# Seven block products for eight in 14 of the 44 weight-tile pairs of the second feed-forward product

## The chip, the cores and the metric

The kernel runs on one core of one Trainium2 chip. The metric is the device time of one execution in microseconds (us). TensorE multiplies matrices, VectorE and ScalarE work on rows of 128 partitions in SBUF and PSUM, GpSimd can do such work too, and SyncE issues the transfers from HBM. TensorE writes only to PSUM, which has eight banks of 128 x 512 numbers.

## The reference

One decoder layer on 256 tokens of width 2048: a token mixer (mLSTM heads and dilated attention), cross-attention into 256 memory tokens, and a SwiGLU feed-forward part. Each of the three is followed by `x = layer_norm(alpha * x + y)` with alpha = 2 ** 0.25. What matters here is the last:

```python
def swiglu_ffn(x, w1, w3, w2):          # x (256, 2048), w1 and w3 (2048, 5632), w2 (5632, 2048)
    return (jax.nn.silu(x @ w1) * (x @ w3)) @ w2
...
    y = swiglu_ffn(x, w1[l], w3[l], w2[l])
    x = layer_norm(DEEPNORM_ALPHA * x + y, ln_g[l, 2], ln_b[l, 2])
```

## The kernel before

All products are computed from float32 values that are split in two: a high part (`SC.copy`, a cast to float32r on ScalarE) and a low part (the value less the high part, a subtraction on VectorE). A product is three matmuls: high x high, high x low and low x high. In a token product (`gemm_tokens`) the transposed activations are the stationary operand, 128 x 128, and a weight tile of 128 rows and 1024 columns moves past it, 512 columns at a time.

The second feed-forward product multiplies the hidden values (`hT`, 44 tiles of 128 features, kept as 22 pairs with both parts) by `w2`. It is done in four pieces. `w2a0` and `w2a1` take the first 24 feature tiles, for the left and the right 1024 output columns; they stand in the middle of the first product, after its piece `f10`. `w2b0` and `w2b1` take the other 20 tiles and come last, before the layer norm. A piece accumulates in four PSUM banks: two halves of the tokens (m) by two halves of its 1024 columns (c). Per weight tile that is 2 x 2 x 3 = 12 matmuls.

`weights` loads the tiles in pairs of 1 MB (three raw buffers, `RAW`) and splits each tile into a pair of buffers `wh` and `wl` (five of each, `SPLIT`). In the last piece the final eight tiles (`LAG2`) are kept in buffers of their own, so that the second token half can follow when the first is already being normed. After a piece `add` puts its four banks into the residual tiles `z`, with the factor alpha in the first pieces and 1.0 in the last; `Norm.add` then takes the statistics too.

`hidden` makes two feature pairs of `hT` from the banks of the first product: silu on ScalarE, a multiplication on VectorE, four transposes on TensorE into a short-lived PSUM bank, and `hT.put`, which splits it. PSUM is shared out as five banks for accumulation (`bank`) and three short-lived ones (`sbank`). SBUF space beside the weight buffers is 34 slots of 128 x 1024, given out in turn (`big`, `slot`, `free`).

The program is written with a scheduler that orders the instructions of each engine ahead of the run, by the order of the text and by when it expects an operand or a buffer to be ready; it also picks the buffers and sets the semaphores. Each engine then works in that order.

Of the kernel before, what the change touches and what calls it, by code (L numbers as in the profile page):

```python
# [35 lines left out]
NSLOT, RAW, SPLIT = 34, 3, 5  # L36
LAG, HEAD, LAG2 = 6, 6, 8
WARM = 2


QM, KM, VM, OM, GI, QA, KA, VA = 0, 1024, 2048, 3072, 4096, 4104, 5128, 6152
# [7 lines left out]
def decoder_layer(ctx: ExitStack, tc: tile.TileContext, A):  # L49
# [48 lines left out]
    def bank(name):  # L98
        return pg.tile([P, 512], F32, tag="g", name=name)
# [18 lines left out]
    class Operand:  # L118


        def __init__(self, name):
            self.name, self.parts = name, {}

        def views(self, j):
            if j not in self.parts:
# [4 lines left out]
        def put(self, j, src):  # L130

            split(*self.views(j), src.rearrange("p (s t) -> p s t", s=2))

        def free(self, j):
            free(self.parts.pop(j))

        def get(self, kt, x, a=0, n=S):
            at = (kt % 2) * 512 + x * S + a
# [30 lines left out]
                split(wh, wl, w[:, s])  # L169
                yield 2 * n + s, wh, wl  # L170

    def weights(src, n, name, load=None, kept=()):

        for b in range(n // 2):
            if load:
                load(b if n == KT else 2 * b)
            first = load is not None and b == 0
            w = wp.tile([P, 2, W], F32, tag="w", name=f"{name}w{b}", bufs=RAW)
            if first:
                for c in range(2):  # L180
                    cs = slice(c * 512, (c + 1) * 512)
                    nc.sync.dma_start(out=w[:, 0, cs], in_=src[b][:, 0, cs])
                if n < KT:
                    load(1)
                nc.sync.dma_start(out=w[:, 1], in_=src[b][:, 1])
            else:
                nc.sync.dma_start(out=w, in_=src[b])
            for i in range(2):
                at = 2 * b + i
                if load and n < KT:  # L190
                    load(at)
                if at in kept:
                    wh, wl = big(f"{name}h{at}"), big(f"{name}l{at}")
                else:
                    wh = wp.tile([P, W], F32R, tag="wh", name=f"{name}h{at}")
                    wl = wp.tile([P, W], F32R, tag="wl", name=f"{name}l{at}")
                eng = G if at in kept and kept[0] == 0 else V
                halves = (slice(0, 512), slice(512, 1024))
                for cs in halves if at in kept or first and i == 0 else (slice(0, 1024),):
                    SC.copy(wh[:, cs], w[:, i, cs])  # L200
                    eng.tensor_tensor(out=wl[:, cs], in0=w[:, i, cs], in1=as_f32(wh[:, cs]), op=ALU.subtract)  # L201
                yield at, wh, wl

    def gemm_tokens(op, src, nkt, name, order=None, kept=range(0), load=None, last=False, steps=None):

        banks = [[bank(f"{name}b{m}{c}") for c in range(2)] for m in range(2)]
        order = order or list(range(nkt))  # L210

        def products(m, n, wh, wl, cols=range(2)):
            xh, xl = (op.get(order[n], x, m * P, P) for x in (0, 1))
            for c in cols:
                cs = slice(c * 512, (c + 1) * 512)
                T.matmul(banks[m][c], xh, wh[:, cs], start=n == 0, stop=False)  # L216
                T.matmul(banks[m][c], xh, wl[:, cs], start=False, stop=False)  # L217
            for c in cols:
                cs = slice(c * 512, (c + 1) * 512)
                T.matmul(banks[m][c], xl, wh[:, cs], start=False, stop=n == nkt - 1)  # L220

        behind = []
        for n, wh, wl in steps or weights(src, nkt, name, load, kept):
            products(0, n, wh, wl)
            if n in kept:
                behind.append((n, wh, wl))
            else:
                products(1, n, wh, wl)
            if kept and n == kept[-1]:
                for c in range(2):  # L230
                    for i, wh, wl in behind:
                        products(1, i, wh, wl, (c,))
                for _, wh, wl in behind:
                    free(wh, wl)
            if last and n % 2 and n not in kept:
                op.free(order[n] // 2)
        if last:
            for n in kept:
                if n % 2:
                    op.free(order[n] // 2)  # L240
        return banks

    def gemm_features(op, src, name, load=None, last=False):
# [277 lines left out]
    def add(m, g, banks, scale=ALPHA):  # L521
        for c in range(2):
            t = z[m][2 * g + c]
            V.scalar_tensor_tensor(out=t, in0=t, scalar=scale, in1=banks[m][c], op0=ALU.mult, op1=ALU.add)

    class Norm:


# [242 lines left out]
    def hidden(j, banks, parts, name):  # L771

        for i in range(2):
# [8 lines left out]
            for s in range(2):  # L782
                for m in range(2):
                    T.transpose(
                        pt[:, s * S + m * P : s * S + (m + 1) * P], hs[m][:, s * P : (s + 1) * P], ident
                    )
            hT.put(j + i, pt)
            free(*hs)

    banks = gemm_tokens(x2, A["w13_tokens"], KT, "f0", kept=range(HEAD))  # L790
# [1 line left out]
    n, half = FFN // 256, 12  # L792

    def w2_first():
        for c in range(2):
            banks = gemm_tokens(hT, A["w2"][c][:half], 2 * half, f"w2a{c}", last=c == 1)
            for m in range(2):
                add(m, c, banks)

    for g in range(2, n, 2):  # L800
        pair = weights_of_pair(A["w13"][g - 2 : g], f"f{g}")
# [4 lines left out]
    ln = Norm(2, "l2")  # L806
    order = list(range(2 * half, HT))
    nkt = len(order)
    banks = gemm_tokens(hT, A["w2"][0][half:], nkt, "w2b0", order)
    for m in range(2):  # L810
        ln.add(m, 0, banks, scale=1.0)
    banks = gemm_tokens(hT, A["w2"][1][half:], nkt, "w2b1", order, kept=range(nkt - LAG2, nkt), last=True)
    for m in range(2):
        ln.add(m, 1, banks, scale=1.0)
        ln.finish(m)
# [102 lines left out]
```

## Time and profile before

| | |
|---|---|
| median of 3 runs | 1573.96 us (1573.64 to 1574.16) |
| the profiled execution | 1573.65 us, of which the span from the first to the last instruction is 1571.7 us |
| TensorE busy | 1556.3 us, 99% of the span, 7554 matmuls |
| VectorE busy | 889.2 us, 57% |
| ScalarE busy | 688.7 us, 44% |
| GpSimd busy | 28.2 us, 2% |
| granted TensorE clock | 0.997 of 2.4 GHz over the span |

The rows give times from the start of the span. PE is TensorE, DVE is VectorE, ACT is ScalarE, POOL is GpSimd. A busy time counts each stretch once, though matmuls overlap.

### The profile page before, as it was taken

To read this page: it belongs to the slowest core of one execution; us is meant where nothing else is said; L and a number is where in the kernel's file an instruction comes from. 1 tells how busy PE (TensorE), PEld (TensorE's weight loads), DVE (VectorE), ACT (ScalarE), POOL (GpSimd) and SP (SyncE) were. 2 spreads that over 40 slices of the span, in tenths; PEclk is the share of its full clock that TensorE was granted. 3 is DMA by queue.
4 is the path that set the end of the run, shared out by engine and by line. 5 is a ranking of instruction groups with operands and counts; after the bars stand their busy time and mean duration, and the time that the engine had idled before them with its cause. 6 is when DMAs were issued, how large, how long until landed. Compare 5 with 4: busy or idle time off the path is not lost.

```text
span 1571.7 us, 18879 instructions
## 1 busy us (share of the span) xinstructions
PE 1556.3 (99%) x7554; PEld 1306.1 (83%) x7554; DVE 889.2 (57%) x1097; ACT 688.7 (44%) x876; POOL 28.2 (2%) x30
## 2 busy tenths in 40 slices
PE   9999999999999999999999999999999999999997
PEld 7888888888888888888887888888888888888886
DVE  5555874586558654555567555445454555545465
ACT  5445554454434544444343444444433344444441
POOL 0000000000000000000023000000000000000000
PEclk9999999999999999999999999999999999999999
DMA  8664455575554555535544655565555665566552
GB/s 297 244 230 171 161 189 185 191 265 182 196 197 162 203 185 187 188 134 193 182 163 160 213 187 187 170 206 191 189 186 209 216 215 187 175 200 198 192 203 77
DMA packets 83349, 301.32 MB, mean 192 GB/s; under 512 B 7181, under 2 KB 9402, under 8 KB 59710
## 3 DMA queue, kind: packets, MB, share of 16 engines
q1 hardware_dynamic: 83262, 300.12, 55.7%
q8 instruction: 59, 0.97, 0.2%
q14 instruction: 28, 0.23, 0.0%
HBM read 297.97 MB, written 4.21 MB: 192 GB/s over the span
## 4 chain that ended last, share of the span: by engine, by line
PE 97%; DVE 2%; DMA 0%; issue 0%; DVEq 0%; ACT 0%; SPq 0%
PE w2a0b L217 1%; PE w2a1b L217 1%; PE w2a0b L216 1%; PE w2a0b L220 1%; PE w2a1b L216 1%; PE w2a1b L220 1%; PE w2b0b L217 1%; PE w2b1b L217 1%; PE w2b0b L220 1%; PE w2b0b L216 1%; PE w2b1b L216 1%; PE w2b1b L220 1%; PE i0b L253 1%; PE i4b L253 1%; PE xq2b L253 1%; PE xq0b L253 1%
## 5 line engine op out<-in xcount | busy, mean ns | idle before, releaser
L201 DVE TENSOR_TENSOR w2a1l<-w2a1w,w2a1h 128x1024 fp32r<-128x1024 f32 x24 | 29.4, 1224 | 32.0 <-ACT w2a1h L200 31.6
L201 DVE TENSOR_TENSOR w2a0l<-w2a0w,w2a0h 128x1024 fp32r<-128x1024 f32 x24 | 29.4, 1225 | 30.8 <-ACT w2a0h L200 30.7
L200 ACT CAST w2a1h<-w2a1w 128x1024 fp32r<-128x1024 f32 x24 | 25.3, 1055 | 40.0 <-PE w2a1b L220 31.6
L200 ACT CAST w2a0h<-w2a0w 128x1024 fp32r<-128x1024 f32 x24 | 25.3, 1055 | 33.9 <-PE w2a0b L220 27.2
L201 DVE TENSOR_TENSOR w2b0l<-w2b0w,w2b0h 128x1024 fp32r<-128x1024 f32 x20 | 24.5, 1225 | 24.9 <-ACT w2b0h L200 24.7
L216 PE MATMUL w2a0b<-w2a0h,hT 128*128 128x512 f32 x96 | 37.5, 391 | 0.0
L217 PE MATMUL w2a0b<-w2a0l,hT 128*128 128x512 f32 x96 | 37.5, 390 | 0.0
L216 PE MATMUL w2a1b<-w2a1h,hT 128*128 128x512 f32 x96 | 37.2, 389 | 0.0
L217 PE MATMUL w2a1b<-w2a1l,hT 128*128 128x512 f32 x96 | 37.2, 389 | 0.0
L200 ACT CAST w2b0h<-w2b0w 128x1024 fp32r<-128x1024 f32 x20 | 21.1, 1055 | 27.2 <-PE w2b0b L220 20.6
L201 DVE TENSOR_TENSOR v2l<-v2w,v2h 128x1024 fp32r<-128x1024 f32 x16 | 19.6, 1224 | 21.9 <-ACT v2h L200 21.9
L201 DVE TENSOR_TENSOR v0l<-v0w,v0h 128x1024 fp32r<-128x1024 f32 x16 | 19.6, 1225 | 21.7 <-ACT v0h L200 21.6
L201 DVE TENSOR_TENSOR w2b1l<-w2b1w,w2b1h 128x512 fp32r<-128x512 f32 (+1 forms) x28 | 24.2, 916 | 13.2 <-ACT w2b1h L200 13.1
L201 DVE TENSOR_TENSOR xv1l<-xv1w,xv1h 128x1024 fp32r<-128x1024 f32 x16 | 19.6, 1225 | 20.7 <-ACT xv1h L200 20.6
L216 PE MATMUL w2b0b<-w2b0h,hT 128*128 128x512 f32 x80 | 31.3, 391 | 0.0
L217 PE MATMUL w2b0b<-w2b0l,hT 128*128 128x512 f32 x80 | 31.2, 390 | 0.0
L200 ACT CAST w2b1h<-w2b1w 128x512 fp32r<-128x512 f32 (+1 forms) x28 | 21.2, 805 | 22.8 <-PE w2b1b L220 10.1
L109 DVE TENSOR_TENSOR f12l<-f12w,f12h 128x1024 fp32r<-128x1024 f32 x16 | 19.6, 1225 | 20.1 <-ACT f12h L108 19.7
L201 DVE TENSOR_TENSOR xv0l<-xv0w,xv0h 128x1024 fp32r<-128x1024 f32 x16 | 19.6, 1225 | 19.9 <-ACT xv0h L200 19.9
L216 PE MATMUL w2b1b<-w2b1h,hT 128*128 128x512 f32 x80 | 30.8, 389 | 0.0
L217 PE MATMUL w2b1b<-w2b1l,hT 128*128 128x512 f32 x80 | 30.8, 389 | 0.0
L109 DVE TENSOR_TENSOR f4l<-f4w,f4h 128x1024 fp32r<-128x1024 f32 x16 | 19.6, 1225 | 18.9 <-ACT f4h L108 18.9
(855 smaller groups left out, 5037.3 us busy)
## 6 DMA issues: line engine op xcount, KB each, us to landing
w2a0w<-in_w SPq DMA_DIRECT2D x12, 1024.0 KB, 4.9
w2a1w<-in_w SPq DMA_DIRECT2D x12, 1024.0 KB, 4.8
w2b0w<-in_w SPq DMA_DIRECT2D x10, 1024.0 KB, 4.8
w2b1w<-in_w SPq DMA_DIRECT2D x10, 1024.0 KB, 4.8
v0w<-in_w_v SPq DMA_DIRECT2D x8, 1024.0 KB, 5.0
v1w<-in_w_v SPq DMA_DIRECT2D x8, 1024.0 KB, 4.9
v2w<-in_w_v SPq DMA_DIRECT2D x8, 1024.0 KB, 4.8
wo0w<-in_w_out SPq DMA_DIRECT2D x8, 1024.0 KB, 4.9
```

What stands on the lines that cost most here:

```text
L109: V.tensor_tensor(out=lo, in0=src, in1=as_f32(hi), op=ALU.subtract)
L200: SC.copy(wh[:, cs], w[:, i, cs])
L201: eng.tensor_tensor(out=wl[:, cs], in0=w[:, i, cs], in1=as_f32(wh[:, cs]), op=ALU.subtract)
L216: T.matmul(banks[m][c], xh, wh[:, cs], start=n == 0, stop=False)
L217: T.matmul(banks[m][c], xh, wl[:, cs], start=False, stop=False)
L220: T.matmul(banks[m][c], xl, wh[:, cs], start=False, stop=n == nkt - 1)
L253: T.matmul(banks[f], wh[:, cs], op.both(kt), start=kt == 0, stop=end, skip_group_check=True)
```

## The change

Fourteen of the 44 pairs of weight tiles (22 pairs for the left and 22 for the right output columns) are multiplied by Winograd's form of Strassen's scheme. A pair of weight tiles by 1024 columns is a 2 x 2 block matrix, and so are two feature tiles by two token halves; seven products of sums of blocks take the place of eight products of blocks. `SEVENS` names the feature pairs. For these, `hidden` copies the transposed values to SBUF and `Operand.mix` makes the four sums of activation blocks, once. `sums` makes the sums of weight blocks on VectorE, in float32, from each raw pair, and splits them: three and a half tiles of 1024 columns in place of two. `gemm_seven` follows a plan in which an integer is a plain pair and a bracketed number one done by seven. It holds five banks (P2, P3, Q4, E, P1) and all three short-lived ones (P5, P7, Q6). After the last bracketed pair of a piece, `early` (from `into_z`) adds the four products that go into several output blocks to `z`; after the piece `add` adds the other banks with the factor 1.0.

```diff
--- before.py
+++ after.py
@@ -37,6 +37,8 @@
 LAG, HEAD, LAG2 = 6, 6, 8
 WARM = 2
+SEVENS = (2, 4, 6, 8, 13, 15, 17)
 QM, KM, VM, OM, GI, QA, KA, VA = 0, 1024, 2048, 3072, 4096, 4104, 5128, 6152
@@ -119,7 +121,7 @@
         def __init__(self, name):
-            self.name, self.parts = name, {}
+            self.name, self.parts, self.mixed = name, {}, {}
         def views(self, j):
             if j not in self.parts:
@@ -131,8 +133,31 @@
             split(*self.views(j), src.rearrange("p (s t) -> p s t", s=2))
+        def mix(self, j, src):
+            d = slot(f"{self.name}d{j}")
+            a11, a21, a12, a22 = (src[:, i * P : (i + 1) * P] for i in range(4))
+            s1, s3, s2, s4 = (d[:, i * P : (i + 1) * P] for i in range(4))
+            V.tensor_tensor(out=s1, in0=a21, in1=a22, op=ALU.subtract)
+            V.tensor_tensor(out=s3, in0=a11, in1=a21, op=ALU.subtract)
+            V.tensor_tensor(out=s2, in0=a11, in1=s1, op=ALU.subtract)
+            V.tensor_tensor(out=s4, in0=a12, in1=s2, op=ALU.subtract)
+            self.mixed[j] = split_rows(d, f"{self.name}m{j}")
+            free(d)
+        def of_product(self, i, j, x):
+            plain = {"P1": (0, 0), "P2": (1, 0), "Q4": (1, P)}
+            if i in plain:
+                s, a = plain[i]
+                return self.get(2 * j + s, x, a, P)
+            at = x * 512 + ("P5", "P7", "Q6", "P3").index(i) * P
+            return self.mixed[j][:, at : at + P]
         def free(self, j):
             free(self.parts.pop(j))
+            if j in self.mixed:
+                free(self.mixed.pop(j))
         def get(self, kt, x, a=0, n=S):
             at = (kt % 2) * 512 + x * S + a
@@ -169,9 +194,9 @@
                 split(wh, wl, w[:, s])
                 yield 2 * n + s, wh, wl
-    def weights(src, n, name, load=None, kept=()):
-        for b in range(n // 2):
+    def weights(src, n, name, load=None, kept=(), blocks=None):
+        for b in range(n // 2) if blocks is None else blocks:
             if load:
                 load(b if n == KT else 2 * b)
             first = load is not None and b == 0
@@ -238,6 +263,90 @@
             for n in kept:
                 if n % 2:
                     op.free(order[n] // 2)
+        return banks
+    def sums(src, b, name):
+        w = wp.tile([P, 2, W], F32, tag="w", name=f"{name}w{b}", bufs=RAW)
+        nc.sync.dma_start(out=w, in_=src[b])
+        t, t2 = big(f"{name}t{b}", F32), big(f"{name}s{b}", F32)
+        q = w.rearrange("p i (c n) -> p (i c) n", c=2)
+        V.tensor_tensor(
+            out=t.rearrange("p (c n) -> p c n", c=2), in0=q[:, 0::3], in1=q[:, 1:2].to_broadcast([P, 2, 512]),
+            op=ALU.add,
+        )
+        V.tensor_tensor(out=t2[:, :512], in0=t[:, :512], in1=q[:, 3], op=ALU.add)
+        V.tensor_tensor(out=t2[:, 512:], in0=t2[:, :512], in1=q[:, 2], op=ALU.add)
+        for to, x, n in (("P1", w[:, 0], 1), (("P2", "P3"), w[:, 1], 2), (("P5", "P7"), t, 2), (("Q6", "Q4"), t2, 2)):
+            wh = wp.tile([P, W], F32R, tag="wh", name=f"{name}h{b}")
+            wl = wp.tile([P, W], F32R, tag="wl", name=f"{name}l{b}")
+            cs = slice(0, 512 * n)
+            split(wh[:, cs], wl[:, cs], x[:, cs])
+            for i, k in enumerate((to,) if n == 1 else to):
+                yield k, wh, wl, slice(i * 512, (i + 1) * 512)
+        free(t, t2)
+    def gemm_seven(op, src, nkt, name, plan, early, order=None, kept=range(0), last=False):
+        order = order or list(range(nkt))
+        of = {i: bank(f"{name}{i}") for i in ("P2", "P3", "Q4", "E", "P1")}
+        of |= {i: sbank(f"{name}{i}") for i in ("P5", "P7", "Q6")}
+        banks = [[of["P2"], of["P3"]], [of["Q4"], of["E"]]]
+        begun = set()
+        final = [b for b in plan if isinstance(b, int)][-1]
+        final7 = [b for b in plan if not isinstance(b, int)][-1][0]
+        def product(to, lhsT, rhs, end):
+            T.matmul(of[to], lhsT, rhs, start=to not in begun, stop=end)
+            begun.add(to)
+        def tile_products(m, n, wh, wl, cols=range(2)):
+            xh, xl = (op.get(order[n], x, m * P, P) for x in (0, 1))
+            for c in cols:
+                cs, to = slice(c * 512, (c + 1) * 512), (("P2", "P3"), ("Q4", "E"))[m][c]
+                product(to, xh, wh[:, cs], False)
+                product(to, xh, wl[:, cs], False)
+            for c in cols:
+                cs, to = slice(c * 512, (c + 1) * 512), (("P2", "P3"), ("Q4", "E"))[m][c]
+                product(to, xl, wh[:, cs], n == 2 * final + 1)
+        behind = []
+        for step in plan:
+            if isinstance(step, int):
+                for n, wh, wl in weights(src, nkt, name, kept=kept, blocks=(step,)):
+                    tile_products(0, n, wh, wl)
+                    if n in kept:
+                        behind.append((n, wh, wl))
+                    else:
+                        tile_products(1, n, wh, wl)
+                b = step
+            else:
+                (b,) = step
+                j = order[2 * b] // 2
+                for to, wh, wl, cs in sums(src, b, name):
+                    xh, xl = (op.of_product(to, j, x) for x in (0, 1))
+                    product(to, xh, wh[:, cs], False)
+                    product(to, xh, wl[:, cs], False)
+                    product(to, xl, wh[:, cs], b == final7 and to in ("P1", "P5", "P7", "Q6"))
+                if b == final7:
+                    early(of)
+            if last and 2 * b not in kept:
+                op.free(order[2 * b] // 2)
+        for c in range(2):
+            for n, wh, wl in behind:
+                tile_products(1, n, wh, wl, (c,))
+        for n, wh, wl in behind:
+            free(wh, wl)
+            if last and n % 2:
+                op.free(order[n] // 2)
         return banks
     def gemm_features(op, src, name, load=None, last=False):
@@ -522,6 +631,25 @@
         for c in range(2):
             t = z[m][2 * g + c]
             V.scalar_tensor_tensor(out=t, in0=t, scalar=scale, in1=banks[m][c], op0=ALU.mult, op1=ALU.add)
+    def into_z(g, scale):
+        def early(of):
+            u, v = slot(f"u{g}"), slot(f"v{g}")
+            SC.copy(u, of["P1"])
+            (z11, z12), (z21, z22) = (z[m][2 * g : 2 * g + 2] for m in range(2))
+            V.scalar_tensor_tensor(out=z11, in0=z11, scalar=scale, in1=of["P1"], op0=ALU.mult, op1=ALU.add)
+            V.tensor_tensor(out=u, in0=u, in1=of["Q6"], op=ALU.subtract)
+            V.tensor_tensor(out=v, in0=of["P5"], in1=u, op=ALU.subtract)
+            V.scalar_tensor_tensor(out=z12, in0=z12, scalar=scale, in1=v, op0=ALU.mult, op1=ALU.add)
+            V.tensor_tensor(out=v, in0=v, in1=of["P7"], op=ALU.subtract)
+            V.scalar_tensor_tensor(out=z22, in0=z22, scalar=scale, in1=v, op0=ALU.mult, op1=ALU.add)
+            V.tensor_tensor(out=u, in0=u, in1=of["P7"], op=ALU.add)
+            V.scalar_tensor_tensor(out=z21, in0=z21, scalar=scale, in1=u, op0=ALU.mult, op1=ALU.add)
+            free(u, v)
+        return early
     class Norm:
@@ -784,7 +912,14 @@
                     T.transpose(
                         pt[:, s * S + m * P : s * S + (m + 1) * P], hs[m][:, s * P : (s + 1) * P], ident
                     )
-            hT.put(j + i, pt)
+            if j + i in SEVENS:
+                h = slot(f"{name}t{i}")
+                SC.copy(h, pt)
+                hT.put(j + i, h)
+                hT.mix(j + i, h)
+                free(h)
+            else:
+                hT.put(j + i, pt)
             free(*hs)
     banks = gemm_tokens(x2, A["w13_tokens"], KT, "f0", kept=range(HEAD))
@@ -792,10 +927,13 @@
     n, half = FFN // 256, 12
     def w2_first():
+        plan = [0, (2,), 1, (4,), 3, (6,), 5, (8,), 7, 9, 10, 11]
         for c in range(2):
-            banks = gemm_tokens(hT, A["w2"][c][:half], 2 * half, f"w2a{c}", last=c == 1)
+            banks = gemm_seven(
+                hT, A["w2"][c][:half], 2 * half, f"w2a{c}", plan, into_z(c, ALPHA), last=c == 1
+            )
             for m in range(2):
-                add(m, c, banks)
+                add(m, c, banks, scale=1.0)
     for g in range(2, n, 2):
         pair = weights_of_pair(A["w13"][g - 2 : g], f"f{g}")
@@ -806,10 +944,13 @@
     ln = Norm(2, "l2")
     order = list(range(2 * half, HT))
     nkt = len(order)
-    banks = gemm_tokens(hT, A["w2"][0][half:], nkt, "w2b0", order)
+    plan = [0, (1,), 2, (3,), 4, (5,), 6, 7, 8, 9]
+    banks = gemm_seven(hT, A["w2"][0][half:], nkt, "w2b0", plan, into_z(0, 1.0), order)
     for m in range(2):
         ln.add(m, 0, banks, scale=1.0)
-    banks = gemm_tokens(hT, A["w2"][1][half:], nkt, "w2b1", order, kept=range(nkt - LAG2, nkt), last=True)
+    plan = [(1,), 0, (3,), 2, (5,), 4, 6, 7, 8, 9]
+    kept = range(nkt - LAG2, nkt)
+    banks = gemm_seven(hT, A["w2"][1][half:], nkt, "w2b1", plan, into_z(1, 1.0), order, kept, True)
     for m in range(2):
         ln.add(m, 1, banks, scale=1.0)
         ln.finish(m)
```

## Rows read from the trace of the kernel before

**Rows 1.** The page: the span, the engines, the last chain by engine.

```profile
span 1571.7 us, 18879 instructions
...
PE 1556.3 (99%) x7554; PEld 1306.1 (83%) x7554; DVE 889.2 (57%) x1097; ACT 688.7 (44%) x876; POOL 28.2 (2%) x30
...
PE 97%; DVE 2%; DMA 0%; issue 0%; DVEq 0%; ACT 0%; SPq 0%
```

**Rows 2.** Waits of TensorE: who waited for whom, us, times, longest.

```profile
PE f0b L220 <- DVE x L109: 1.8, 1, 1.8
...
PE x2p L567 <- DVE z L556: 0.6, 1, 0.6
```

**Rows 3.** Busy time by stretch: f10, then w2a0, w2a1, w2b0, w2b1.

```profile
core 0: us, PE busy (x) PEld busy (x) DVE busy (x) ACT busy (x) POOL busy (x), PEclk, DMA share, GB/s
1054.00:1098.47 44.47, 44.47 (x202) 36.80 (x201) 22.24 (x23) 19.15 (x23) 0.00 (x0) 1.00 0.57 189
1098.47:1164.70 66.23, 66.23 (x298) 54.82 (x297) 31.99 (x31) 26.90 (x28) 0.00 (x0) 1.00 0.55 191
1164.70:1229.96 65.26, 65.26 (x289) 54.05 (x288) 31.69 (x29) 25.32 (x24) 0.00 (x0) 1.00 0.58 201
1451.40:1506.75 55.35, 55.35 (x250) 45.81 (x249) 27.09 (x27) 22.68 (x24) 0.00 (x0) 1.00 0.55 190
1506.75:1561.30 54.55, 54.55 (x241) 44.85 (x239) 33.26 (x48) 16.98 (x24) 0.91 (x1) 1.00 0.37 135
```

**Rows 4.** Timeline of TensorE in w2a1: start, us, instruction.

```profile
1176.93 0.39 PE L216 MATMUL w2a1b<-w2a1h,hT 128*128 128x512 f32 x1
...
1179.65 0.39 PE L216 MATMUL w2a1b<-w2a1h,hT 128*128 128x512 f32 x1
```

**Rows 5.** Groups of VectorE by shape: busy us, mean ns, idle before.

```profile
L201 DVE TENSOR_TENSOR w2a1l<-w2a1w,w2a1h 128x1024 fp32r<-128x1024 f32 x24 | 29.4, 1224 | 32.0 <-ACT w2a1h L200 31.6
L201 DVE TENSOR_TENSOR w2b1l<-w2b1w,w2b1h 128x512 fp32r<-128x512 f32 x16 | 10.0, 687 | 2.8 <-ACT w2b1h L200 2.8
L109 DVE TENSOR_TENSOR x<-x2p,x 128x256 fp32r<-128x256 f32 x16 | 6.1, 412 | 4.4 <-ACT x L108 4.3
L551 DVE SCALAR_TENSOR_TENSOR z<-z,l2mv,f20h 128x512 f32<-128x512 f32 x2 | 1.4, 742 | 0.0
L556 DVE SCALAR_TENSOR_TENSOR z<-z,l1r,l1b 128x512 f32<-128x512 f32 x4 | 4.9, 1252 | 0.0
```

**Rows 6.** Groups of ScalarE by shape.

```profile
L200 ACT CAST w2a1h<-w2a1w 128x1024 fp32r<-128x1024 f32 x24 | 25.3, 1055 | 40.0 <-PE w2a1b L220 31.6 <-PE w2a0b L220 8.3
L200 ACT CAST w2b1h<-w2b1w 128x512 fp32r<-128x512 f32 x16 | 8.7, 618 | 4.4 <-DMA w2b1w<-in_w 4.4
```

**Rows 7.** DMA issues: count, KB each, median us to landing.

```profile
w2a0w<-in_w SPq DMA_DIRECT2D x12, 1024.0 KB, 4.9
```

**Rows 8.** Timeline of VectorE from the end of w2a0.

```profile
1163.31 0.69 DVE L524 SCALAR_TENSOR_TENSOR xk1r<-xk1r,w2a0b 128x512 f32<-128x512 f32 x1 [1.54 <-PE w2a0b L220]
1163.91 1.22 DVE L201 TENSOR_TENSOR w2a1l<-w2a1w,w2a1h 128x1024 fp32r<-128x1024 f32 x1
1165.05 0.68 DVE L524 SCALAR_TENSOR_TENSOR xk1r<-xk1r,w2a0b 128x512 f32<-128x512 f32 x1
```

**Rows 9.** Timeline of ScalarE at the start of w2a1.

```profile
1164.89 1.05 ACT L200 CAST w2a1h<-w2a1w 128x1024 fp32r<-128x1024 f32 x1 [1.67 <-PE w2a0b L220]
1171.69 1.05 ACT L200 CAST w2a1h<-w2a1w 128x1024 fp32r<-128x1024 f32 x1 [5.75 <-PE w2a1b L220]
```

**Rows 10.** Timeline of VectorE in w2a0.

```profile
1104.63 1.29 DVE L109 TENSOR_TENSOR hT<-f10p,hT 128x512 fp32r<-128x512 f32 x2 [3.34 <-ACT hT L108]
```

**Rows 11.** Busy time by stretch around TensorE's 1.8 us wait.

```profile
823.00:826.00 3.00, 2.24 (x16) 1.69 (x15) 3.00 (x2) 2.88 (x7) 3.00 (x3) 1.00 0.32 76
826.00:830.00 4.00, 2.16 (x8) 1.44 (x7) 3.97 (x12) 1.58 (x4) 4.00 (x4) 0.88 0.49 205
830.00:835.00 5.00, 5.00 (x21) 3.98 (x20) 5.00 (x4) 1.72 (x3) 5.00 (x4) 0.76 0.62 213
```

## The prediction

> **What bounds the kernel now.** I read the page first, then the waits of TensorE, then a table of the stretches that hold the second feed-forward product, then the timelines of the engines there. TensorE is busy for 1556.3 of the span's 1571.7 us and the chain that ended last lies on it for 97% [rows 1]. Its longest wait on another engine is 1.8 us, and none of its few waits is in the second product [rows 2]. In the four stretches of that product TensorE is busy for the whole window at the full granted clock, 2.4 GHz, while VectorE works 48%, 49%, 49% and 61% of it and ScalarE 31% to 41% (31.99 of 66.23 us and so on) [rows 3]. So a product block less is time less, as long as VectorE and ScalarE deliver operands in time.
>
> **The price of one matmul.** A 128x512 matmul shows 0.39 us, but they overlap: twelve of them go from 1176.93 to 1179.65, 0.2267 us each [rows 4]. The stretch of 1164.70 to 1229.96 holds the 288 of one half product: 65.26/288 = 0.2266 [rows 3]. The Trainium skill (TensorE: Matmul & The Clock Gate, "Back-to-back issue gap") gives about 216 ns for 512 columns at the full clock; by it the term below would be an estimated 9.06 us. The rows say 227 ns, and I keep to them.
>
> **What goes.** A pair of weight tiles is 2 tiles x 2 token halves x 2 column halves x 3 matmuls (high x high, high x low, low x high) = 24 matmuls. By seven products it is 21. Fourteen pairs save 42: 42 x 0.2266 = 9.5 us, all on the path. Nothing is added to TensorE: every term has the same three matmuls of 512 columns, and weight loads stay one for one.
>
> **What comes: VectorE and ScalarE in the seven-product pairs.** Now a pair costs VectorE two 1024-wide subtractions, 2 x 1.224 = 2.45 us, and ScalarE 2 x 1.055 = 2.11 [rows 5, 6]. A seven has one 1024-wide and two 512-wide additions, then splits of 512 and three times 1024: VectorE 1.224 + 2 x 0.687 + 0.687 + 3 x 1.224 = 6.96 us, ScalarE 0.618 + 3 x 1.055 = 3.78 [rows 5, 6]. No row shows an addition with a broadcast operand. Below, I take the same element count, 1.224; above, 128x512 ops that ran at 1.252 in place of 0.742 us while GpSimd was also at work, which would add (1.252/0.742 - 1) x 2.6 = 1.8 us a pair [rows 5]. GpSimd is idle in these stretches (0.00, but for 0.91 near the end) [rows 3], so I take the lower.
>
> TensorE needs 21 x 0.2266 = 4.76 us for a seven and 5.44 for a plain pair. VectorE alone could not follow a row of sevens (6.96 against 4.76), but the plans alternate: 10.20 us of TensorE against 9.41 of VectorE and 5.89 of ScalarE. VectorE goes from half busy to 92% with 0.8 us to spare per two pairs, and where the alternation ends come four or five plain pairs with 3.0 us to spare each.
>
> **Is an operand late?** Operands pass through five buffers for high and five for low parts. ScalarE waits for TensorE to give one back, VectorE for ScalarE: 31.6 us each in the second half product, of 32.0 and 40.0 idle before these groups [rows 5, 6]. So work runs ahead as far as the buffers allow. A refill is 0.19 us to see the release (w2a0 ends at 1164.70, the cast starts at 1164.89 [rows 9]), 1.055 cast, 1.224 subtraction: 2.5 us. A buffer's need comes after the four tiles ahead of it. The tightest is the first tile behind a seven, covered by four shorter products, 4.76 us, which leaves 2.26 us for other VectorE work in front. If all three additions of the next seven (2.6 us) stand there, TensorE waits 0.35 us; 14 times that is 4.9 us. The additions need only the raw tile, three of which are in flight and land 4.9 us after issue [rows 7], so they can run in VectorE's waits. I take 0 inside the alternation, and keep 4.9 for the range.
>
> At the change of half products the lead shrinks. Four additions into the residual (0.68 each) wait for TensorE's end, and TensorE takes a first bank's products of several tiles before it finishes any; after the cast at 1164.89 ScalarE sat 5.75 us until TensorE gave a buffer back, at 1171.7, 7.0 us after the start at 1164.7 [rows 8, 9]. Five buffers hold 13.6 us of plain tiles, so that cost nothing. Now they hold two plain tiles and the first three of a seven: 5.44 + 0.68 + 1.36 + 1.36 = 8.84 us. A refill begun at 7.0 is ready at 9.3, about 0.5 us late, with the next ones close behind at VectorE's 92%. I count 1.0 us each at the starts of w2a1 and w2b1: 2.0 in all, 0 below.
>
> **The early additions.** After the last seven of each half product VectorE does eight 512-wide operations, five with an operand in PSUM and three without, 5 x 0.68 + 3 x 0.742 = 5.6 us [rows 5, 8]. ScalarE's copy beside them is about 0.6. By the refill sums two plain tiles are then ready, 5.4 us of cover, and the third would be late by up to 5.6 + 1.2 - 5.4 = 1.4 us if all eight stood ahead of it. The first needs only P1, done earlier, and the scheduler put subtractions between the residual's additions in the kernel before (1163.91, between two of them) [rows 8]. I take 0; bound 4 x 1.4 = 5.6.
>
> **Work moved to the first product.** Seven hidden pairs get a copy, a cast, four 128x128 subtractions and one 512-wide one. VectorE: from 0.687 at 512 and 0.412 at 256 wide, 0.27 at 128 is my estimate: 4 x 0.27 + 0.69 = 1.8 us; ScalarE 0.6 + 0.6 [rows 5, 6]. VectorE is idle for 22.2 of 44.47 us in such a stretch [rows 3], and four to five tiles of 2.72 us stand ready: nothing. Without that cover it would be 7 x 3.0 = 21 us. DMA moves the same bytes in another order at 0.55 to 0.58 of its time in three of the four stretches, 0.37 in the last [rows 3]: nothing. PSUM is full in a seven-product stretch, eight banks of eight. In w2a0 and w2b0 two of them still hold the last transposes; VectorE frees them 7.45 us after the start (1104.63 + 1.29 against 1098.47) [rows 10], and the second of the short banks is wanted after the plain pair, the transposes (66.23 - 65.26) [rows 3] and P1, P2, P3 and P5: 5.44 + 0.97 + 2.72 = 9.1. Nothing again, by 1.7 us. The end after the last matmul is unchanged.
>
> **Sum.** The profiled execution took 1573.65 us, its span 1571.7 and 1.95 around it; the median of the runs is 1573.96, 0.3 above. 1573.65 - 9.5 + 2.0 = 1566.1.
>
> **Rivals.**
> Some of the gain comes back at every seven: additions ahead of the tile behind a seven (4.9) with the 2.0 above: 1571.0. For it: VectorE at 92%, in order. Against: the raw tiles are early.
> The early additions become the wait, on the other side of no change: if no split tile is ready when VectorE begins its eight operations, TensorE waits 5.6 + 1.2 = 6.8 us, four times: 1573.65 - 9.5 + 27.2 = 1591.4. It decides at 2.4 us a place, that is, with fewer than 1.6 tiles (2.72 us each) ready. For it: the first operands VectorE reads end just as the seven does, and VectorE has sat 3.34 us in front of an operation whose input came late [rows 10]. Against: two tiles by my count.
> VectorE is the bound: with 1.8 us more a pair (the upper price) it needs 11.2 against 10.2, 14 us over fourteen: 1578.
> The clock falls. In the stretch around the 1.8 us wait [rows 2] it read 0.88 for 4 us and 0.76 for 5: 0.96 + 2.4 = 3.4 us at 1.2 GHz, a loss of 1.7 us [rows 11]. Four waits of such a size in the second product would cost 4 x (1.8 + 1.7) = 14 us: 1578. Against: it takes waits that I don't forecast; a shorter one (0.6, in 823 to 826) left the clock at 1.00 [rows 2, 11]. The Trainium skill (the same page, "A second HAM failure mode: psum-queue depth-cycling") says that frequent small idle moments between groups of matmuls through changing PSUM banks can make the clock oscillate; by that rule the time would be this rival's, and the trace agrees only for the long wait.
> That the change leaves TensorE's work as it was is excluded: 42 matmuls are not issued.
>
> **How the numbers follow.** About 0.2% (3.1 us) is what a measurement of this kernel can tell from no change. My forecast, with waits of 0 to 4.5 us (1564.1 to 1568.6), gets 0.62. Waits of 4.5 to 6.4 us, most of them the first rival, 0.14. That it takes back all of it to within 0.2%, 0.13. Slower 0.11: the early additions 0.06, VectorE as the bound 0.03, the clock 0.02. So faster 0.76, same 0.13, slower 0.11. The range starts just under the case with no wait, 1563.9, and reaches into the third case, to 1571.5, leaving out 2 in 10.
>
> **What would show it.** 7512 matmuls for 7554. The w2a0, w2a1, w2b0 and w2b1 stretches shorter by 2.7, 2.7, 2.0 and 2.0 us less their waits (12, 12, 9, 9 matmuls). VectorE about 90% busy in the alternation, the group of 1024-wide additions at 1.22 us, TensorE's waits named after the low parts and near the starts of w2a1 and w2b1. I am wrong if TensorE shows waits of over 2 us behind VectorE after each last seven, if the additions take over 1.5 us, or if the clock reads under 1.00 there.

## The result, and the profile after

The changed kernel takes 1564.53 us (median of 4 runs, 1563.84 to 1564.84) against 1573.87 of the kernel before on the same chip, a ratio of 0.994 with the interval 0.9923 to 0.9957: 9.3 us less. The forecast was 1566.1, 1.6 more. One run of experiment 5 took 1712.9 us at a granted clock of 0.85 over its span; it is left out of the times below. A second measurement, beside the last experiments, gave 1564.44 (0.994, 0.9928 to 0.9953).

The page after, beside [rows 1]:

```profile
span 1562.7 us, 18965 instructions
...
PE 1544.3 (99%) x7512; PEld 1295.7 (83%) x7512; DVE 971.1 (62%) x1234; ACT 717.0 (46%) x922; POOL 28.3 (2%) x30
```

42 matmuls fewer, 82 us more of VectorE, and the span 9.0 us shorter. The stretches of [rows 3] after the change, f10, w2a0, w2a1, w2b0 and w2b1 (columns as there):

```profile
1054.40:1098.80 44.40, 44.40 (x201) 36.77 (x200) 25.13 (x31) 19.48 (x24) 0.00 (x0) 1.00 0.57 190
1098.80:1162.40 63.60, 63.60 (x286) 52.55 (x284) 52.22 (x59) 33.24 (x37) 0.00 (x0) 1.00 0.55 199
1162.40:1225.00 62.60, 62.60 (x278) 51.84 (x277) 50.14 (x54) 31.90 (x33) 0.00 (x0) 1.00 0.58 202
1446.40:1499.70 53.30, 53.30 (x240) 44.08 (x239) 45.42 (x53) 27.30 (x31) 0.00 (x0) 1.00 0.57 198
1499.70:1552.10 52.40, 52.40 (x232) 43.18 (x231) 46.04 (x65) 22.29 (x31) 0.91 (x1) 1.00 0.38 134
```

The first three pieces are shorter by 2.6, 2.7 and 2.0 us, and the last, from its first matmul to its last, by 2.0; 12, 12, 9 and 9 matmuls at 0.2266 are 2.7, 2.7, 2.0 and 2.0. TensorE is busy for the whole of each at full clock. The stretches together give 9.3 us; the span falls by 9.0, because the work in front of f10 stood 0.3 us later already in its first stage, i0b, before any changed instruction. That is loading: ScalarE's first casts of i0's weights wait for their transfers a little longer each, and TensorE waits 1.6 us for them in place of 0.5. The list of TensorE's waits names nothing in the second product, as in [rows 2]. After the change, and the i0b row of the kernel before:

```profile
PE f0b L242 <- DVE f0l L226: 2.0, 2, 1.6
PE f0b L245 <- DVE x L111: 1.8, 1, 1.8
PE i0b L362 <- ACT i0h L225: 1.6, 2, 0.8
```

```profile
PE i0b L253 <- ACT i0h L200: 0.5, 1, 0.5
```

The f0b rows are no loss against the kernel before: its 1.8 us wait was the same, and the clock fell behind it where the changed kernel waits for f0l (last section).

The new operations of VectorE, by shape, beside [rows 5]:

```profile
L278 DVE TENSOR_TENSOR w2a1t<-w2a1w 128x1024 f32<-128x1024 f32 x4 | 4.9, 1221 | 0.0
L282 DVE TENSOR_TENSOR w2a1s<-w2a1t,w2a1w 128x512 f32<-128x512 f32 x4 | 2.8, 689 | 0.1
L111 DVE TENSOR_TENSOR w2a1l<-w2a1t,w2a1h 128x1024 fp32r<-128x1024 f32 x4 | 4.9, 1218 | 0.0
```

The addition with a broadcast operand takes what a subtraction of that size takes, the lower of the two prices. The alternations alone, one row for each piece:

```profile
1098.80:1138.00 39.20, 39.20 (x178) 32.35 (x177) 31.71 (x36) 22.55 (x27) 0.00 (x0) 1.00 0.52 188
1162.40:1202.00 39.60, 39.60 (x176) 32.82 (x175) 33.03 (x36) 22.21 (x24) 0.00 (x0) 1.00 0.53 186
1446.40:1478.00 31.60, 31.60 (x145) 26.08 (x144) 25.69 (x30) 19.25 (x23) 0.00 (x0) 1.00 0.49 167
1499.70:1531.00 31.30, 31.30 (x139) 25.91 (x139) 29.56 (x38) 20.11 (x27) 0.00 (x0) 1.00 0.56 198
```

VectorE is busy for 81%, 83%, 81% and, in w2b1, 94%. The timeline of VectorE shows why 92% was too much in the first three, and where the early additions went. From w2a1, behind its last seven:

```profile
1201.09 0.68 DVE L642 SCALAR_TENSOR_TENSOR z<-z,w2a1P 128x512 f32<-128x512 f32 x1
1201.69 2.35 DVE L226 TENSOR_TENSOR w2a1l<-w2a1w,w2a1h 128x1024 fp32r<-128x1024 f32 x2
1203.96 0.68 DVE L643 TENSOR_TENSOR u<-u,w2a1Q 128x512 f32<-128x512 f32 x1
1204.56 2.35 DVE L226 TENSOR_TENSOR w2a1l<-w2a1w,w2a1h 128x1024 fp32r<-128x1024 f32 x2
...
1212.22 0.69 DVE L649 SCALAR_TENSOR_TENSOR z<-z,u 128x512 f32<-128x512 f32 x1
```

Two subtractions of 1.22 us end after 2.35: the next one starts 1.13 to 1.14 us after the first. An operation of 512 columns is followed 0.60 us later (1201.09 to 1201.69). So a seven costs VectorE 4 x 1.14 + 3 x 0.60 = 6.4 us in its queue, not 6.96, and two pairs 8.6 of 10.2. The eight early additions are spread from 1201.1 to 1212.2 between the splits of the plain pairs, never in front of them as one block.

### The profile page after: what moved, and what is told of

The parts are those of the page before. It is cut to its first block, busy times and chain, and to the rows that moved or that the text cites. A ratio compares the mean times of both kernels' runs of the same rounds, so it can differ in the third digit from the quotient of the medians.

```text
span 1562.7 us, 18965 instructions
## 1 busy us (share of the span) xinstructions
PE 1544.3 (99%) x7512; PEld 1295.7 (83%) x7512; DVE 971.1 (62%) x1234; ACT 717.0 (46%) x922; POOL 28.3 (2%) x30
## 4 chain that ended last, share of the span: by engine, by line
PE 97%; DVE 2%; DMA 1%; issue 0%; SPq 0%; ACT 0%; DVEq 0%
PE w2a0P L308 2%; PE w2a1P L308 2%; PE w2b0P L308 2%; PE w2b1P L308 2%; PE w2a0Q L308 1%; PE w2a1Q L308 1%; PE i4b L362 1%; PE xq2b L362 1%; PE xq0b L362 1%; PE i6b L362 1%; PE xq1b L362 1%; PE xk2b L362 1%; PE xq3b L362 1%; PE i3b L362 1%; PE i1b L362 1%; PE xk1b L362 1%
## 5 line engine op out<-in xcount | busy, mean ns | idle before, releaser
L226 DVE TENSOR_TENSOR xv1l<-xv1w,xv1h 128x1024 fp32r<-128x1024 f32 x16 | 19.6, 1225 | 20.7 <-ACT xv1h L225 20.6
L111 DVE TENSOR_TENSOR f20l<-f20w,f20h 128x1024 fp32r<-128x1024 f32 x16 | 19.6, 1225 | 18.9 <-ACT f20h L110 18.7
L111 DVE TENSOR_TENSOR f2l<-f2w,f2h 128x1024 fp32r<-128x1024 f32 x16 | 19.6, 1225 | 18.7 <-ACT f2h L110 18.6
L226 DVE TENSOR_TENSOR wo0l<-wo0w,wo0h 128x1024 fp32r<-128x1024 f32 x16 | 19.6, 1226 | 18.7 <-ACT wo0h L225 18.5
L226 DVE TENSOR_TENSOR xo0l<-xo0w,xo0h 128x1024 fp32r<-128x1024 f32 x16 | 19.6, 1225 | 18.4 <-ACT xo0h L225 18.4
L111 DVE TENSOR_TENSOR f8l<-f8w,f8h 128x1024 fp32r<-128x1024 f32 x16 | 19.5, 1224 | 17.7 <-ACT f8h L110 17.7
L111 DVE TENSOR_TENSOR f10l<-f10w,f10h 128x1024 fp32r<-128x1024 f32 x16 | 19.5, 1224 | 17.7 <-ACT f10h L110 17.7
L111 DVE TENSOR_TENSOR f6l<-f6w,f6h 128x1024 fp32r<-128x1024 f32 x16 | 19.5, 1224 | 17.7 <-ACT f6h L110 17.7
L111 DVE TENSOR_TENSOR f14l<-f14w,f14h 128x1024 fp32r<-128x1024 f32 x16 | 19.6, 1225 | 17.6 <-ACT f14h L110 17.6
L111 DVE TENSOR_TENSOR f18l<-f18w,f18h 128x1024 fp32r<-128x1024 f32 x16 | 19.6, 1225 | 17.6 <-ACT f18h L110 17.6
L111 DVE TENSOR_TENSOR f16l<-f16w,f16h 128x1024 fp32r<-128x1024 f32 x16 | 19.6, 1225 | 17.6 <-ACT f16h L110 17.6
```

What stands on the lines that cost most here:

```text
L111: V.tensor_tensor(out=lo, in0=src, in1=as_f32(hi), op=ALU.subtract)
```

## The experiments

The times are medians; the kernel before stood at 1573.75 to 1573.93 us on the chips that ran them. Differences of under 0.5 us between runs are not read.

**1. No additions.** The three `V.tensor_tensor` lines of `sums` are left out (one makes t, two make t2) and raw blocks split, so P5, P7, Q6 and Q4 are products of other weights than the reference's:

```diff
-        V.tensor_tensor(out=t..., in0=q[:, 0::3], in1=q[:, 1:2]...)
-        ... (("P5", "P7"), t, 2), (("Q6", "Q4"), t2, 2) ...
+        ... (("P5", "P7"), w[:, 0], 2), (("Q6", "Q4"), w[:, 1], 2) ...
```

> The three additions of weight blocks are left out of all fourteen pairs done by seven; the splits take raw blocks in their place, so the output is not the layer's. TensorE's work and the splits stay. Theory (the additions lie wholly beside TensorE's work): 1564.5 us, within 0.5. Rival (VectorE holds TensorE up somewhere in the alternation, so that the additions' 33 us of VectorE are partly on the path): over 0.5 us faster than the changed kernel, below 1564.0, towards the 1563.9 of no wait at all or less.

Measured: 1564.15 us (1563.89 to 1564.36), within what the theory allowed. The additions cost some 0.4 us at most, which is not clear of the noise; they are hidden.

**2 and 3. The additions twice, and three times.**

```diff
+        for _ in range(2):
             V.tensor_tensor(out=t..., ...)
...
```

The loop stands around all three additions; in the second of the two kernels it is `range(3)`.

> Each of the three additions of a pair done by seven is issued twice, with the same result. Back to back in the changed kernel a 1024-wide operation starts 1.14 us and a 512-wide one 0.60 us after the one before it, less than their shown durations of 1.22 and 0.69. Theory A (those distances are what an operation costs VectorE: 8.6 of 10.2 us per plain pair and seven): with 2.3 more it needs 11.0, 0.8 too many, mostly taken up by the lead of the buffers: 1564.5 to 1568.5 us. Theory B (the durations cost, as in the prediction's 9.4 of 10.2): 12.0 against 10.2, 1.8 us at each of fourteen, less some 12 us of lead in four pieces: about 1577 us.

> Each of the three additions is issued three times, with the same result. Theory A (distances of 1.14 and 0.60 us): 13.3 us of VectorE against 10.2 of TensorE for each plain pair and seven; 3.1 x 14 = 44 us, less a lead of 4 to 5 us in each of four pieces: 20 to 30 us above the changed kernel, 1585 to 1595 us. Theory B (durations): 14.6 against 10.2, 62 us less some 16: about 1610 us. A rival without a limit by VectorE expects under 1570 us.

Measured: 1575.55 us (1573.81 to 1576.24, 10 runs) and 1602.34 (1601.71 to 1606.01). Both totals lie between the theories. By pieces, three additions make w2a0, w2a1 and w2b0 longer than in the changed kernel by 7.5, 10.1 and 4.8 us. Theory A gives 3.1 x 4 - 4.5 = 7.9, 7.9 and 4.8, theory B 13, 13 and 9: nearer to A, though neither counted the clock, which took some 1.5 us in each (0.98, 0.98 and 0.97 below). Experiment 5 shows the distances directly. w2b1 lost 15.8, and 8.6 with the additions twice, where A expected little. The four pieces with three additions, by stretch:

```profile
1098.90:1170.00 71.10, 67.10 (x285) 52.93 (x284) 67.14 (x80) 32.40 (x37) 0.00 (x0) 0.98 0.51 178
1170.00:1242.70 72.70, 66.61 (x277) 52.27 (x276) 67.44 (x76) 31.18 (x33) 0.00 (x0) 0.98 0.51 174
1464.10:1522.20 58.10, 55.81 (x240) 44.66 (x239) 56.84 (x69) 24.98 (x29) 0.00 (x0) 0.97 0.47 168
1522.20:1590.40 68.20, 58.74 (x232) 46.01 (x230) 60.12 (x82) 24.27 (x33) 0.92 (x1) 0.90 0.35 124
```

TensorE idles 9.5 of 68.2 us in the last, and the mean clock of 0.90 means 0.2 x 68.2 = 13.6 us at 1.2 GHz, another 6.8 lost. The clock did in w2b1 what the fourth rival said, once there were waits.

**4. Eighteen sevens.**

```diff
-SEVENS = (2, 4, 6, 8, 13, 15, 17)
+SEVENS = (2, 4, 6, 8, 10, 13, 15, 17, 21)
-plans ..., (8,), 7, 9, 10, 11] / ..., (5,), 6, 7, 8, 9] / ..., (5,), 4, 6, 7, 8, 9], kept 12 to 19
+plans ..., (8,), 7, (10,), 9, 11] / ..., (5,), 6, (9,), 7, 8] / ..., (5,), 4, (9,), 6, 7, 8], kept 12 to 17
```

> Eighteen pairs by seven in place of fourteen: pair 10 as well in both first pieces, the pair of tiles 18 and 19 of the last pieces (feature pair 21) in both last pieces; six weight tiles are kept for the second token half at the end in place of eight. Theory (TensorE's count sets the time, VectorE has room at 8.6 of 10.2 us): 12 matmuls less x 0.2266 = 2.7 us: 1561.8 us, up to 0.8 more at the end, where less work of the second token half covers the norm of the first. Rival (VectorE is at its limit): nothing gained or a loss, 1564 us or more.

Measured: 1572.22 us (11 runs), 7.7 above the changed kernel: the expectation was wrong. w2a1 took 62.0 us, 0.6 less, as forecast. w2a0 took 68.7 in place of 63.6. TensorE, ScalarE and VectorE near its start (timelines):

```profile
1112.51 0.80 PE L308 MATMUL w2a0Q<-w2a0h,hTm 128*128 128x512 f32 x1 [4.00 <-ACT w2a0h L110]
```

```profile
1108.58 0.62 ACT L110 CAST hTm<-f10h 128x512 fp32r<-128x512 f32 x1 [2.88 <-DVE f10h L144]
1111.41 1.05 ACT L110 CAST w2a0h<-w2a0s 128x1024 fp32r<-128x1024 f32 x1 [2.21 <-DVE w2a0s L283]
```

```profile
1104.10 1.22 DVE L278 TENSOR_TENSOR w2a0t<-w2a0w 128x1024 f32<-128x1024 f32 x1 [2.74 <-PE f10p L912]
```

The sums of weight blocks waited 2.74 us for a slot that the last hidden values held until they were transposed, and the activation sums of pair 10 stood in both queues before the cast that TensorE needed. The clock fell with that wait (0.83 over 1110 to 1120). The rest is at the end: w2b0 and w2b1 together take 1.5 us more in spite of six matmuls less, and 12.5 us pass behind their last matmul in place of 10.6. How these parts come about was not tried one by one.

**5. The sevens in a row.**

```diff
-plans 0, (2,), 1, (4,), 3, (6,), 5, (8,), 7, ... / 0, (1,), 2, (3,), 4, (5,), 6, ... / (1,), 0, (3,), 2, (5,), 4, 6, ...
+plans 0, 1, (2,), (4,), (6,), (8,), 3, 5, 7, ... / 0, 2, (1,), (3,), (5,), 4, 6, ... / (1,), (3,), (5,), 0, 2, 4, 6, ...
```

> The same fourteen pairs by seven, but in a row in each piece and not in turn with plain pairs; everything else as in the changed kernel. Theory (the turn is what hides VectorE's work): a seven takes VectorE 6.4 us by the distances between its operations against 4.76 of TensorE, 1.6 short; four in a row lose 6.4 less the lead of the buffers, 4 to 5 us, so 1 to 3 us in w2a0, w2a1 and w2b0 each, and 3 to 6 in w2b1, which begins with three sevens while the residual's additions and statistics are done: 1568 to 1577 us. Rival (the order of the pairs is of no account, the lead or the scheduler hides it): 1564.5 us, within 1.

Measured: 1565.36 us (1565.12 to 1565.60, 3 runs), pieces of 63.5, 62.6, 53.3 and 52.3 us: the theory falls. The turn with plain pairs isn't needed. VectorE in w2a0 (by stretch, then three rows of its timeline):

```profile
1098.70:1109.00 10.30, 10.30 (x51) 8.49 (x50) 6.45 (x12) 4.21 (x7) 0.00 (x0) 1.00 0.28 102
1109.00:1128.00 19.00, 19.00 (x86) 15.71 (x84) 19.00 (x22) 14.12 (x17) 0.00 (x0) 1.00 0.55 179
```

```profile
1092.96 1.22 DVE L278 TENSOR_TENSOR w2a0t<-w2a0w 128x1024 f32<-128x1024 f32 x1
...
1098.41 1.22 DVE L278 TENSOR_TENSOR w2a0t<-w2a0w 128x1024 f32<-128x1024 f32 x1
...
1106.01 1.22 DVE L278 TENSOR_TENSOR w2a0t<-w2a0w 128x1024 f32<-128x1024 f32 x1
```

The additions go into slots of their own and need only a raw tile, so three of the four wide ones were made before the run of sevens began, outside the five buffers that my lead of 4 to 5 us counted. Through the four sevens VectorE is busy for 19.00 of 19.00 us, and TensorE doesn't wait: it just fits. This stretch also gives the price of VectorE's work. From 1108.94 to 1127.92, 18.98 us, twenty operations run without a gap, thirteen of 1024 columns and seven of 512: 13 x 1.135 + 7 x 0.60 = 19.0 by distances, 20.7 by durations.

**6. The last seven at the end of the piece**, in w2a0, w2a1 and w2b0 (and the last matmul of P2, P3 and Q4 marked there):

```diff
-plans ..., (8,), 7, 9, 10, 11] / ..., 4, (5,), 6, 7, 8, 9]
+plans ..., 7, 9, 10, 11, (8,)] / ..., 4, 6, 7, 8, 9, (5,)]
```

> In w2a0, w2a1 and w2b0 the last pair done by seven is moved to the end of the piece, so that no plain pairs follow the early additions; w2b1 stays. Theory (the early additions, 5.6 us by durations, are hidden by the four plain pairs behind them): without these they stand together with the four of the residual before the next piece gets its banks; TensorE waits 1 to 4 us at each of the three changes: 1567 to 1577 us. Rival (the scheduler finds room for them anywhere): 1564.5 us, within 1.

Measured: 1576.58 us (10 runs), 12.1 above the changed kernel, as the theory said in sum; at its three places w2a1 is 3.4 longer, f12 0.8, w2b1 7.0, where it gave 1 to 4 each. Two waits of TensorE, and the stretches around the second:

```profile
1171.68 0.50 PE L309 MATMUL w2a1Q<-w2a1h,hTm 128*128 128x512 f32 x1 [1.66 <-DVE f10h L649]
...
1509.03 0.50 PE L309 MATMUL w2b1P<-w2b1l,hT 128*128 128x512 f32 x1 [1.89 <-DVE w2b1l L226]
```

```profile
1504.00:1512.00 8.00, 5.60 (x19) 3.22 (x17) 7.93 (x10) 2.00 (x2) 0.00 (x0) 0.92 0.48 152
1512.00:1520.00 8.00, 7.60 (x23) 5.74 (x23) 8.00 (x13) 2.88 (x4) 0.00 (x0) 0.65 0.26 111
```

Line 649 is the last early addition that reads a bank: TensorE stood until the bank was given up. The second wait is for a low part that VectorE made late. The place of the last seven is worth more than the 9.3 us of the whole change. In w2b1 the clock took 0.08 x 8 + 0.35 x 8 = 3.4 us of the 7.0.

**7 and 8. Four buffers in place of five**, in the changed kernel and in the one before:

```diff
-NSLOT, RAW, SPLIT = 34, 3, 5
+NSLOT, RAW, SPLIT = 34, 3, 4
```

> The changed kernel with four buffers for the high and four for the low parts of weight tiles in place of five, in the whole kernel. Theory (the lead of the buffers hides VectorE's uneven work): with 3 tiles ahead the first tile behind a seven is covered by 4.08 us against a refill of 2.5, and any addition in front makes it late: 3 to 10 us more than its own counterpart loses, 1568 to 1575 us. Rival (the lead is of no account beyond the first tiles): no more than the kernel before loses by the same cut.

> The kernel before with four buffers in place of five, as the counterpart. Both theories: VectorE is half idle there and a refill of 2.5 us stands against 8.2 us of cover by three plain tiles, so only the changes between products can lose: 1574 to 1577 us.

Measured: 1568.80 us (7 runs) and 1575.07 (10 runs): 4.3 and 1.3 us. Some 1.2 us are lost by both in the other products; the other 3.0 are all in w2b1 (55.4 us in place of 52.4), at the lower edge of what the theory said. In the second product the fifth buffer is needed there only. By the count of its matmuls 1.0 us is lost within 10 us of the start of w2b1 and 2.0 at its last seven (1525 to 1530). VectorE and TensorE there:

```profile
1527.39 0.68 DVE L642 SCALAR_TENSOR_TENSOR z<-z,w2b1P 128x512 f32<-128x512 f32 x1
1527.99 0.68 DVE L643 TENSOR_TENSOR u<-u,w2b1Q 128x512 f32<-128x512 f32 x1
1528.59 2.35 DVE L226 TENSOR_TENSOR w2b1l<-w2b1w,w2b1h 128x1024 fp32r<-128x1024 f32 x2
```

```profile
1529.86 0.74 PE L308 MATMUL w2b1P<-w2b1l,hT 128*128 128x512 f32 x2 [0.82 <-DVE w2b1l L226]
```

Two early additions stand in front of the low part that TensorE waits for: with a shorter lead, this is the rival of the early additions, in one place.

**9. Seventeen sevens**, without the three burdens of the eighteen:

```diff
+SEVENS = (2, 4, 6, 8, 9, 13, 15, 17, 19)
+plans ..., (8,), 7, (9,), 10, 11] / ..., (5,), 6, (7,), 8, 9], w2b1 as in the changed kernel
```

> Seventeen pairs by seven: pair 9, whose activation sums are made one step of the first product earlier than those of pair 10, as a fifth in both first pieces, pair 7 of the last ones as a fourth in w2b0; w2b1 and its eight kept tiles stay. Theory (with eighteen the loss came from sums of activations made at the very start of w2a0, from the shorter work behind the first token half at the end and from the crowded start of w2b1, not from VectorE's load as a whole): 9 matmuls less than the changed kernel, 2.0 us: 1562.5 us, up to 1 more if the additions again wait for a slot in w2a0. Rival (VectorE or the space of the slots is at its limit with fourteen): 1565 us or more.

Measured: 1567.78 us (1567.52 to 1568.75), 3.3 above: the expectation was wrong. w2a0 took 62.8 and w2a1 62.0: 0.8 and 0.6 us less, as counted. The loss, some 5 us against the count, is in w2b1. Half of it lies at its start, where the longest wait of TensorE is at 1504.39, and half at its last seven (1521 to 1533):

```profile
1504.39 0.73 PE L308 MATMUL w2b1P<-w2b1l,hT 128*128 128x512 f32 x2 [1.33 <-DVE w2b1l L226]
```

The early additions of w2b0, with two plain pairs behind them, now end at 1501.92, 13.8 us later than in the changed kernel (1488.14), among the sums for the start of w2b1. That two plain pairs are too few is read from this; no run changed it alone, and the space of the slots was not ruled out.

**10. The additions twice, w2b1 beginning with a plain pair.**

```diff
-    plan = [(1,), 0, (3,), 2, (5,), 4, 6, 7, 8, 9]
+    plan = [0, (1,), 2, (3,), 4, (5,), 6, 7, 8, 9]
```

> The additions issued twice as before, but w2b1 begins with a plain pair, as w2b0 does, and not with a seven. Theory (of the 11 us that the doubled additions cost, the 8.6 in w2b1 come from its start, where the residual's four additions and four statistics meet two sevens and one plain pair): 6 to 8 us less than with the sevens first, 1567 to 1570 us. Rival (VectorE's load over the whole alternation is what costs): within 2 us of 1575.5.

Measured: 1573.02 us (10 runs), 2.5 less than experiment 2; expected were 6 to 8, and the rival's 2 is missed too. In the profiled execution, at 1575.00 us the longest of the ten, w2b1 itself fell by 4.7 us, to 56.3, but 3.8 came back after its last matmul. VectorE near the end:

```profile
1548.92 0.69 DVE L644 TENSOR_TENSOR u<-u,w2b1Q 128x512 f32<-128x512 f32 x1 [4.07 <-PE w2b1Q L309]
```

The last seven now ended so late that the early additions stood before the layer norm. So its start is a part of what w2b1 is short of, and its end the other; 3.9 us are still lost, all within 18 us of its first matmul.

**11. The additions on GpSimd.**

```diff
-        V.tensor_tensor(
+        G.tensor_tensor(
```

So for each of the three in `sums`.

> The three additions of weight blocks of all fourteen pairs are made on GpSimd in place of VectorE. A 128x512 subtraction took GpSimd some 1.3 to 1.6 us in the kernel before, so a pair needs 5 to 6 us of GpSimd, in 10.2. Theory (contention, as in the upper price of the prediction: VectorE's operations take 1.25 in place of 0.74 us while GpSimd works): half of VectorE's time in the alternation stretches by up to 1.7, which is more than the additions relieve it of: 1567 to 1580 us. Rival (GpSimd simply takes the load off VectorE): 1564.3 us, within 0.5.

Measured: 1565.59 us (1564.87 to 1565.83), between the two, and clear of both: w2b1 is 1.1 us longer, the others are unchanged. The groups of GpSimd and of VectorE:

```profile
L282 POOL TENSOR_TENSOR w2a1s<-w2a1t,w2a1w 128x512 f32<-128x512 f32 x4 | 8.6, 2157 | 0.3
```

```profile
L226 DVE TENSOR_TENSOR w2a1l<-w2a1w,w2a1h 128x1024 fp32r<-128x1024 f32 x16 | 25.3, 1608 | 4.3 <-ACT w2a1h L225 4.3
```

The contention is there, 1.61 us in the mean for 1.22, but what VectorE no longer has to do about pays for it: it is busy for 52.0 us of w2a0 as against 52.2.

**12. The changed kernel again.**

> The changed kernel again, unaltered, beside the seventeen on the same chip: 1564.5 us, within 0.5, by every theory.

Measured: 1564.44 us (1563.98 to 1564.79).

## Why the prediction was right, and where it was off

- **What goes**: right. 42 matmuls at 0.2266 are 9.5 us; the pieces got 9.3 shorter.
- **What comes**: right in that it hides (experiment 1). VectorE's load was priced too high: durations overlap by 0.08 to 0.09 us from one operation to the next, so 8.6 of 10.2 us, not 9.4. Experiment 5 shows by twenty operations in a row that the distances are what counts.
- **Inside the alternation**: 0 was right, and for the reason that was given: the additions run in VectorE's waits. In w2a1 two of the three do stand in front of the tile behind a seven, but that tile's cast waits meanwhile until TensorE returns a buffer. It ends at 1179.5 (the row holds two casts), and the tile's subtraction starts 0.1 us later. ScalarE, then VectorE:

```profile
1178.46 2.01 ACT L225 CAST w2a1h<-w2a1w 128x1024 fp32r<-128x1024 f32 x2 [1.89 <-PE w2a1E L308]
```

```profile
1177.75 1.22 DVE L278 TENSOR_TENSOR w2a1t<-w2a1w 128x1024 f32<-128x1024 f32 x1
1179.00 0.69 DVE L282 TENSOR_TENSOR w2a1s<-w2a1t,w2a1w 128x512 f32<-128x512 f32 x1
1179.61 1.22 DVE L226 TENSOR_TENSOR w2a1l<-w2a1w,w2a1h 128x1024 fp32r<-128x1024 f32 x1
```

- **The start of w2a1 and w2b1**: the term that was off, 2.0 us forecast, none visible. The step that failed is that TensorE gives the first buffer back 7.0 us after the start, as in [rows 9]. Now it is 4.3 us in w2a1 (start at 1162.40). ScalarE there:

```profile
1162.64 1.05 ACT L110 CAST w2a1h<-w2a1t 128x1024 fp32r<-128x1024 f32 x1 [1.71 <-PE w2a0E L308]
1166.68 1.06 ACT L110 CAST w2a1h<-w2a1s 128x1024 fp32r<-128x1024 f32 x1 [2.98 <-PE w2a1P L308]
```

A buffer of P1 or of P2 and P3 is free again after three or six matmuls and not after twelve: 18 matmuls go before the first return, where it was 30. The tile cast at 1166.68 has its low part at 1168.99, and TensorE takes it up at 1171.24 (VectorE, then TensorE):

```profile
1167.76 1.23 DVE L111 TENSOR_TENSOR w2a1l<-w2a1s,w2a1h 128x1024 fp32r<-128x1024 f32 x1 [0.26 <-ACT w2a1h L110]
```

```profile
1171.24 0.39 PE L308 MATMUL w2a1Q<-w2a1h,hTm 128*128 128x512 f32 x1
```

Without this term the time lies 0.6 us above the lower end of the range, 1563.9, the end that stands for no wait. Where there are losses the start counts, but not alone: of what w2b1 loses, it has 1.0 of 3.0 us in experiment 7, half in 9 and 3.9 of 8.6 in 2; the rest lies at its last seven.

- **The early additions**: 0 was right; VectorE's queue holds them in ones, twos and threes between the splits. The rival's mechanism is real: experiment 7 shows it as it was put, a split part late behind early additions. Without plain pairs behind the last seven the loss is 12.1 us (experiment 6), of which a part is a wait for a bank, which the prediction did not count.
- **The clock**: 1.00 in all four pieces, as forecast. It took its part of the losses in experiments 2, 3, 4, 6 and 10, and none in 7, 9 and 11. The rival's price of 1.7 us is right where the clock falls, but the same wait does not always make it fall (last section).

## What to carry to other kernels

Where TensorE never waits, a matmul that isn't issued is worth its start-to-start distance, and additions on another engine are free as long as their queue time, read from the distances between back-to-back operations, fits between the points where that engine must wait. Give such additions buffers of their own, so that they can run ahead of the buffers that TensorE returns. Look for the tight places at the change from one accumulation to the next and behind the last seven: in experiment 9 two plain pairs less behind a seven came with a loss larger than what the product saved. From experiment 9, five sevens in each of w2a0 and w2a1 with w2b0 and w2b1 left alone should give 1.4 us more; that kernel was not run.

## What the runs showed of the hardware

The clock's part of the losses was larger than I had thought. After waits of TensorE of 1.75 us (experiment 10) and 4.00 us (experiment 4) a stretch of 10 us read 0.83: 3.4 us at 1.2 GHz, 1.7 lost each time, as in [rows 11]. In experiment 9 the 1.33 us wait left it at 1.00, and in experiment 6 a wait of 1.66 in w2a1 did too. The length of one wait doesn't decide it. The 1.8 us wait at the start of f0 stands in all fourteen profiles, 1.83 to 1.86 us long; in nine the clock fell behind it as in [rows 11], and in five it stayed at 1.00. The changed kernel's is one of the five:

```profile
826.00:830.00 4.00, 2.17 (x9) 1.45 (x9) 3.97 (x10) 1.46 (x5) 4.00 (x3) 1.00 0.55 223
830.00:835.00 5.00, 5.00 (x25) 4.11 (x24) 5.00 (x5) 2.06 (x3) 5.00 (x5) 1.00 0.58 210
```

In those five TensorE then waited 1.6 us for the f0l operand, some 9 us later, so nothing was gained. What decides is open.

GpSimd and VectorE slowed each other while both worked in experiment 11: 128x512 on GpSimd mostly took 2.16 us, and 1.29 in f0 while VectorE was idle; for 128x1024 on VectorE, 1.22 us otherwise, the 1.61 is a mean over sixteen operations, some of them with GpSimd idle.
